# A convolution block's sums in the spare PSUM banks, two loads swapped, and five more warm-up transposes

## The chip, the cores and the metric

The kernel runs on one core of a Trainium2 chip. The metric is the device time of one execution in microseconds (us). The engines are TensorE (PE in the profile; its weight loads are PEld), VectorE (DVE), ScalarE (ACT), GpSimd (POOL) and SyncE (SP), which here only issues loads.

## What is computed

One layer of a hybrid encoder on a sequence of 256 rows and 2048 columns, in float32:

```python
xn = rms_norm(h, norm1_g)
proj = xn @ w_in                      # 2048 x 5120: q, k, v, and the convolution's ga, gg
...                                   # attention on q, k, v gives att
u = ga * sigmoid(gg)                  # 1024 channels
u = causal_depthwise_conv(u, conv_w, conv_b)      # 31 taps along the sequence
u = silu(layer_norm(u, conv_ln_g, conv_ln_b))
h = h + concat([att, u]) @ w_out
hn = rms_norm(h, norm2_g)
h = h + (silu(hn @ w_gate) * (hn @ w_up)) @ w_down
```

## The kernel before

**Products.** Each float32 matrix is cut into a rounded part (`hi`) and a rest (`lo`), and a product is the sum of three matmuls: hi by hi, hi of the weights by lo of x (lines 368 and 369), and lo of the weights by hi of x (line 374). A weight chunk is 512 KB. SP loads it (`raw`), ScalarE casts it to `whi` (line 329), and VectorE takes the difference as `wlo` (line 338). TensorE does the first half of a chunk from `whi` and the second from `wlo`.

**Blocks.** `w_in` is worked through in blocks of columns, each summed over all 2048 rows into two PSUM banks, one for each half of the 256 sequence rows. The first five blocks are those of the convolution: `CONV_BLOCKS = (1, 1, 2, 2, 2)` tiles of 128 channels, with both `gg` and `ga` columns. So blocks 1 and 2 have 256 columns and blocks 3 to 5 have 512. Block 1 has five chunks, block 2 four, block 3 eight.

**Banks.** PSUM has eight banks. Four are the pool `acc_ps`, from which blocks take two in turn (`accs[key]` in `multiply`). Four are the pool `aux_ps`, for transposes, attention scores and the like. `held` counts the banks of the second pool that are in longer use; whoever wants one waits with `room` until the count allows it. A block with `spare=True` takes its two banks from `aux_ps` and adds two to `held`. Before, only parts of the output projection did so, and block 3 followed block 1 in its two banks.

**What happens to a block's sums.** `glu_done` runs when a block is summed. It waits until the row norm of x (`rstd1`, from the squares of x on ScalarE, a reduction on VectorE in line 513 and a power on GpSimd in line 213) is known, takes the sigmoid of the `gg` half on ScalarE (line 539), and multiplies on VectorE (line 544, tile `u`). These two read the block's banks. Then TensorE transposes `u` (line 552), ScalarE copies it (line 553) and makes the first tap (line 557), and VectorE adds the other thirty (line 564).

**What sets the order.** The program is written out in order. Such followers are generators: `resume` lets each go one step, twice a chunk, so they stand in each engine's queue at fixed places between the chunks. `run_side` puts taps between the splits, by a budget of VectorE's time.

**The start.** ScalarE's queue issues the first part of x transposed (`xt`), then the norm columns (`cols`: gains and biases, 29 KB); SP's issues weights and the rest of x. ScalarE scales x by a column of `cols` (line 235, `lhi`), VectorE makes the rest (line 236, `llo`). Meanwhile TensorE transposes the identity matrix `WARM` times.

Of the kernel before, what the change touches and what calls it, by code (L numbers as in the profile page):

```python
# [22 lines left out]
NM = S // P  # L23
# [25 lines left out]

NK = 2  # L50

WARM = 14

XPARTS = (range(0, 2), range(2, 4), range(4, 8), range(8, 12), range(12, 16))

# [53 lines left out]
def tile_block(  # L109
# [6 lines left out]
    act, dve, pool, pe, sp = nc.scalar, nc.vector, nc.gpsimd, nc.tensor, nc.sync  # L116
# [23 lines left out]
    def warm_up(n):  # L140
        warm = aux_ps.tile([P, N], F32, tag="aux", name="ps_warm")
        for _ in range(n):
            pe.transpose(warm[:, :P], ident, ident)

    warm_up(WARM)

    cols = once.tile([P, NR], F32, tag="cols", name="cols")
    halves_of_x = [early.tile([P, HK, S], F32, tag="wb", name="xt") for _ in range(2)]

    def x_load(ks, queue):  # L150
        i, k = divmod(ks[0], HK)
        n = len(ks)
        queue.dma_start(out=halves_of_x[i][:, k : k + n].rearrange("p k s -> p (k s)"),
                        in_=xt[:, ks[0] * S : (ks[0] + n) * S])

    x_load(XPARTS[0], act)
    act.dma_start(out=cols, in_=gains)

    act.copy(small.tile([P, 8], F32, tag="rsq", name="first"), neghalf)

    def col(key, k):
        return cols[:, AT[key] + k : AT[key] + k + 1]
# [88 lines left out]
    def lag(n):  # L251
        for _ in range(n):
            yield


    held = [0]

    def room(n, hold=0):
        while held[0] + n > AUX:
            yield  # L260
        held[0] += hold
# [6 lines left out]
    def spend(us):  # L268
        credit[0] -= us
# [19 lines left out]
    def block(w, cols, ks, xs, done=None, bkey=None, first=True, last=True, spare=False, cuts=()):  # L289

        ks = list(ks)
        cols = [(cols, N)] if isinstance(cols, int) else cols
        width = sum(n for _, n in cols)
        bkey = bkey if bkey is not None else ("b", len(chunks))
        i = 0
        cuts = list(cuts)
        while i < len(ks):
            part = ks[i : i + (cuts.pop(0) if cuts else NK * N // width)]
            i += len(part)
            chunks.append(dict(w=w, k0=part[0], nk=len(part), cols=cols, width=width, xs=xs, bkey=bkey,  # L300
                               first=part[0] == ks[0] and first, last=last and i == len(ks),
                               done=done if i == len(ks) else None, spare=spare, by_dma=False,
                               load=load_chunk, round=round_chunk,
                               split=split_chunk, multiply=multiply))
# [222 lines left out]
        pool.memset(upad[b][:, :, : W - 1], 0.0)  # L527
    y = pre.tile([P, NCT, S], F32, tag="y", name="y", bufs=1)

    def glu_done(c0, nct, ps):  # L530

        w = nct * P
        while not normed:
            yield
        yield
        sig = []
        for m in range(NM):
            sig.append(pre.tile([P, HN], F32, tag="p1", name="sig"))
            act.activation(sig[m][:, :w], ps[m][:, :w], AF.Sigmoid, scale=rstd1[m])
        yield from lag(2)  # L540
        us = []
        for m in range(NM):
            u = pre.tile([P, HN], F32, tag="wt", name="u", bufs=4)
            dve.scalar_tensor_tensor(u[:, :w], ps[m][:, w:], rstd1[m], sig[m][:, :w], ALU.mult, ALU.mult)  # L544
            us.append(u)
        spend(0.25)
        yield from lag(3)
        yield from room(1)
        pt = aux_ps.tile([P, 2, S], F32, tag="aux", name="ps_u")
        for j in range(nct):  # L550
            for m in range(NM):
                pe.transpose(pt[:, j, m * P : (m + 1) * P], us[m][:, j * P : (j + 1) * P], ident)
        act.copy(upad[c0 // NB][:, c0 % NB : c0 % NB + nct, W - 1 :], pt[:, :nct])
        yield
        cts = range(c0, c0 + nct)
        for ct in cts:
            act.activation(y[:, ct, :], upad[ct // NB][:, ct % NB, :S], AF.Identity,
                           bias=col("cb", ct), scale=cw[:, ct, :1])
            side.append(deque((lambda k=k, ct=ct: tap(k, ct)) for k in range(1, W)))

    def tap(k, ct):
        src = upad[ct // NB][:, ct % NB, k : k + S]
        wk = cw[:, ct, k : k + 1]
        dve.scalar_tensor_tensor(y[:, ct, :], src, wk, y[:, ct, :], ALU.mult, ALU.add)  # L564
        if k == W - 1:
            tapped[ct // NB] += 1
            if tapped[ct // NB] == NB:
                start(conv_back(ct // NB))
# [647 lines left out]
    c0 = 0  # L1216
    for nct in CONV_BLOCKS:
        block("w_in", [(GC + c0 * P, nct * P), (AC + c0 * P, nct * P)], range(KD), fx,
              lambda ps, c0=c0, nct=nct: glu_done(c0, nct, ps), cuts=[len(p) for p in XPARTS] if c0 == 0 else ())
        c0 += nct  # L1220
    for b in range(2):
        block("w_in", KC + b * N, range(KD), fx, lambda ps, b=b: qk_done("k", b, ps))
# [67 lines left out]
```

## Time and profile before

| | us |
|---|---|
| median of 3 runs | 1061.22 (1060.52 to 1062.36) |
| the profiled execution: its time | 1062.85 |
| its span in the profile | 1061.1 |
| PE busy | 1036.1 (98%) |
| DVE busy | 882.1 (83%) |
| ACT busy | 667.4 (63%) |
| POOL busy | 138.1 (13%) |

A row of a time line gives the start in us from the span's start, the length in us, the engine, the line, the operation, what it writes and reads, and how many equal instructions the row joins (then the length runs from the first's start to the last's end). In brackets stands the idle time of the engine before it and what ended that. A row of a table by stretches gives each engine's busy time in the stretch with the number of its instructions in brackets, then the TensorE clock that was granted (PEclk, 1.00 is full), the DMA engines' busy share and what they moved in GB/s. A row of loads gives the median time from issue to landing at its end.

### The profile page before, as it was taken

To read this page: it belongs to the slowest core of one execution; us is meant where nothing else is said; L and a number is where in the kernel's file an instruction comes from. 1 tells how busy PE (TensorE), PEld (TensorE's weight loads), DVE (VectorE), ACT (ScalarE), POOL (GpSimd) and SP (SyncE) were. 2 spreads that over 40 slices of the span, in tenths; PEclk is the share of its full clock that TensorE was granted. 3 is DMA by queue.
4 is the path that set the end of the run, shared out by engine and by line. 5 is a ranking of instruction groups with operands and counts; after the bars stand their busy time and mean duration, and the time that the engine had idled before them with its cause. 6 is when DMAs were issued, how large, how long until landed. Compare 5 with 4: busy or idle time off the path is not lost.

```text
span 1061.1 us, 13189 instructions
## 1 busy us (share of the span) xinstructions
PE 1036.1 (98%) x4734; PEld 856.6 (81%) x4734; DVE 882.1 (83%) x1103; ACT 667.4 (63%) x850; POOL 138.1 (13%) x182
## 2 busy tenths in 40 slices
PE   8799999999999999999999999999999999999998
PEld 8688888878778887787888888888888888888776
DVE  5499999989766489989979679899896697989984
ACT  6554457756567466676765566775865556668661
POOL 0030022211200100010101120100101111001021
PEclk9899999999999999999999999999999999999999
DMA  9556555454546668987969998979878999879985
GB/s 361 204 170 200 193 180 171 159 170 147 164 155 198 213 211 257 310 235 231 321 196 292 283 301 265 293 212 324 238 238 259 297 280 333 244 233 275 282 219 117
DMA packets 63186, 250.20 MB, mean 236 GB/s; under 512 B 7184, under 2 KB 8208, under 8 KB 55696
## 3 DMA queue, kind: packets, MB, share of 16 engines
q1 hardware_dynamic: 48224, 201.34, 53.2%
q0 software_dynamic: 14608, 47.72, 23.2%
q8 instruction: 37, 0.61, 0.2%
q10 hardware_dynamic: 288, 0.29, 0.1%
q14 instruction: 29, 0.24, 0.1%
HBM read 240.94 MB, written 8.39 MB: 235 GB/s over the span
## 4 chain that ended last, share of the span: by engine, by line
PE 55%; DVE 6%; issue 2%; ACT 1%; DMA 0%; POOL 0%; DVEq 0%; ACTq 0%; POOLq 0%
PE q L1069 10%; PE q L1070 10%; PE q L1074 10%; PE q L1048 8%; PE q L1049 7%; PE q L1050 7%; DVE wl L1031 1%; DVE wl L1030 1%; DVE wt L1019 1%; PE ps_a L886 1%; DVE wlo L338 1%; PE acc L374 1%; PE acc L369 1%; PE acc L368 1%; DVE wt L1020 0%
## 5 line engine op out<-in xcount | busy, mean ns | idle before, releaser
L329 ACT CAST whi<-raw 128x1024 fp32r<-128x1024 f32 (+1 forms) x261 | 268.8, 1046 | 114.5 <-PE q L1070 48.5
L338 DVE TENSOR_TENSOR wlo<-raw,whi 128x1024 fp32r<-128x1024 f32 (+1 forms) x188 | 227.4, 1217 | 97.5 <-ACT whi L329 97.4
L368 PE MATMUL acc<-whi,lhi 128*128 128x512 f32 (+1 forms) x448 | 169.5, 383 | 9.6 <-DVE u L544 6.9
L369 PE MATMUL acc<-whi,llo 128*128 128x512 f32 (+1 forms) x448 | 167.4, 379 | 0.0
L1026 ACT CAST wh<-wt 128x2048 fp32r<-128x2048 f32 x58 | 110.8, 1910 | 38.1 <-DVE wt L1021 37.8
L1031 DVE TENSOR_TENSOR wl<-wt,wh 128x2048 fp32r<-128x2048 f32 x58 | 132.7, 2287 | 1.8 <-ACT wh L1026 0.9
L333 POOL DMA_DIRECT2D wlo<-in_wts_dram x73 | 63.9, 875 | 521.8 <-ACT wlo L332 480.4
L1030 DVE TENSOR_TENSOR wl<-wb,wh 128x1536 fp32r<-128x1536 f32 x58 | 101.7, 1753 | 29.6 <-ACT wh L1025 29.4
L1069 PE MATMUL q<-whi,chi 128*128 128x512 f32 x320 | 125.3, 392 | 0.0
L1070 PE MATMUL q<-whi,clo 128*128 128x512 f32 x320 | 124.6, 389 | 0.0
L374 PE MATMUL acc<-wlo,lhi 128*128 128x512 f32 (+1 forms) x448 | 115.2, 382 | 1.5 <-DVE wlo L338 1.5
L1048 PE MATMUL q<-wh,fhi 128*128 128x512 f32 x280 | 109.8, 392 | 3.1 <-DVE sum L1150 1.4
L1050 PE MATMUL q<-wl,fhi 128*128 128x512 f32 x280 | 109.0, 389 | 0.0
L1049 PE MATMUL q<-wh,flo 128*128 128x512 f32 x280 | 109.0, 389 | 0.0
L368 PEld LDWEIGHTS acc<-whi,lhi 128*128 128x128 f32 x448 | 86.0, 192 | 25.3 <-issue 7.0
L564 DVE SCALAR_TENSOR_TENSOR y<-upad,cw,y 128x256 f32<-128x256 f32 x240 | 103.2, 481 | 0.3
L369 PEld LDWEIGHTS acc<-whi,llo 128*128 128x128 f32 x448 | 86.0, 192 | 15.0
L1025 ACT CAST wh<-wb 128x1536 fp32r<-128x1536 f32 x58 | 85.5, 1474 | 18.0 <-PE q L1049 9.9
L374 PEld LDWEIGHTS acc<-wlo,lhi 128*128 128x128 f32 x448 | 80.7, 191 | 16.8 <-DVE wlo L338 2.4
L1074 PE MATMUL q<-wlo,chi 128*128 128x512 f32 x320 | 86.3, 391 | 0.0
L332 ACT ACTIVATE wlo<-raw 128x1024 fp32r<-128x1024 f32 x73 | 77.2, 1057 | 0.0
L1019 DVE TENSOR_TENSOR wt<-wb 128x1024 f32<-128x1024 f32 x58 | 70.8, 1220 | 0.9 <-DMA wb<-in_wts_dram 0.4
(208 smaller groups left out, 1679.8 us busy)
## 6 DMA issues: line engine op xcount, KB each, us to landing
raw<-in_wts_dram SPq DMA_DIRECT2D x259, 512.0 KB, 5.4
wb<-in_wts_dram SPq DMA_DIRECT2D x57, 1024.0 KB, 7.5
wlo<-in_wts_dram POOLq DMA_DIRECT2D x73, 512.0 KB, 9.0
out_dram<-sum POOLq DMA_DIRECT2D x22, 256.0 KB, 7.0
h<-in_x_dram SPq DMA_DIRECT2D x4, 512.0 KB, 8.8
out_dram<-h POOLq DMA_DIRECT2D x8, 256.0 KB, 5.5
xt<-in_xt_dram SPq DMA_DIRECT2D x3, 512.0 KB, 7.4
wb<-in_wts_dram POOLq DMA_DIRECT2D x1, 1024.0 KB, 8.0
```

The costliest lines, as they stand in the source:

```text
L329: act.copy(c["hi"], c["raw"])
L338: dve.tensor_tensor(c["lo"], c["raw"], c["hi"].bitcast(F32), ALU.subtract)
L368: pe.matmul(ps[m], xhi[:, ms], hi[:, j, :], start=c["first"] and j == 0, stop=False)
L369: pe.matmul(ps[m], xlo[:, ms], hi[:, j, :], start=False, stop=False)
L374: pe.matmul(ps[m], xhi[:, ms], lo[:, j, :], start=False, stop=c["last"] and j == nk - 1)
L1031: dve.tensor_tensor(c["lo"][:, :4], c["t"], c["hi"][:, :4].bitcast(F32), ALU.subtract)
L1048: pe.matmul(ps, fhi[:, f, p, :], c["hi"][:, w], start=bool(first), stop=False)
L1049: pe.matmul(ps, flo[:, f, p, :], c["hi"][:, w], start=False, stop=False)
L1050: pe.matmul(ps, fhi[:, f, p, :], c["lo"][:, w], start=False, stop=bool(last))
L1069: pe.matmul(ps, plain[i][0][:, ms], hi[:, i, :], start=i == 0 and bool(c["first"].get(qs[m])), stop=False)
L1070: pe.matmul(ps, plain[i][1][:, ms], hi[:, i, :], start=False, stop=False)
L1074: pe.matmul(sum_bank(c, qs[m]), plain[i][0][:, ms], lo[:, i, :], start=False, stop=i == 1 and bool(c["last"].get(qs[m])))
```

## The change

Three things. Block 3 (`c0 == 2`) gets `spare=True`: it sums in two banks of `aux_ps`, and `glu_done` gives these back in `held` once `u` is written. ScalarE's queue issues the norm columns ahead of the first part of x. `WARM` is 19 in place of 14.

```diff
-WARM = 14
+WARM = 19
...
+    act.dma_start(out=cols, in_=gains)
     x_load(XPARTS[0], act)
-    act.dma_start(out=cols, in_=gains)
...
-    def glu_done(c0, nct, ps):
+    def glu_done(c0, nct, ps, spare):
...
             us.append(u)
+        if spare:
+            held[0] -= NM
         spend(0.25)
...
         block("w_in", [(GC + c0 * P, nct * P), (AC + c0 * P, nct * P)], range(KD), fx,
-              lambda ps, c0=c0, nct=nct: glu_done(c0, nct, ps), cuts=[len(p) for p in XPARTS] if c0 == 0 else ())
+              lambda ps, c0=c0, nct=nct: glu_done(c0, nct, ps, c0 == 2),
+              cuts=[len(p) for p in XPARTS] if c0 == 0 else (), spare=c0 == 2)
```

On every engine the instructions stand in the same order as before, but for the swapped loads and the number of warm-ups; what changes are the banks and with them the waits. (Lines behind the change have numbers higher by 2 or 3.) The head of ScalarE's queue, before (-) and now (+):

```order
-L1281 UNCONDITIONAL_BRANCH
+L1284 UNCONDITIONAL_BRANCH
+L156 DMA cols<-in_gains_dram 128x58
 L153 DMA xt<-in_xt_dram 128x512
-L157 DMA cols<-in_gains_dram 128x58
 L159 ACT_TABLE_LOAD
 L159 COPY first<-neghalf 128x8
```

The two loads have changed places, and nothing else has moved there. TensorE's queue where block 2 ends and block 3 begins, with the engines that an instruction waits for in brackets (`acc_324` and `acc_325` are block 2's banks, `acc_481` and `acc_482` block 3's, which before are those of block 1); before:

```order
L374 MATMUL acc_324<-wlo_363,lhi_90 128x256 [waits DVE_49]
L374 MATMUL acc_324<-wlo_363,lhi_90 128x256 x3
L374 MATMUL acc_325<-wlo_363,lhi_90 128x256 x4
L368 MATMUL acc_481<-whi_399,lhi_90 128x512 [waits DVE_49,PE_49,Activation_49]
L369 MATMUL acc_481<-whi_399,llo_91 128x512
L368 MATMUL acc_482<-whi_399,lhi_90 128x512 [waits DVE_49,PE_49,Activation_49]
L369 MATMUL acc_482<-whi_399,llo_91 128x512
```

The same place now (block 2 has `acc_329` and `acc_330`, block 3 `acc_486` and `acc_487`):

```order
L374 MATMUL acc_329<-wlo_368,lhi_90 128x256 [waits DVE_49]
L374 MATMUL acc_329<-wlo_368,lhi_90 128x256 x3
L374 MATMUL acc_330<-wlo_368,lhi_90 128x256 x4
L368 MATMUL acc_486<-whi_404,lhi_90 128x512 [waits Activation_49]
L369 MATMUL acc_486<-whi_404,llo_91 128x512
L368 MATMUL acc_487<-whi_404,lhi_90 128x512
L369 MATMUL acc_487<-whi_404,llo_91 128x512
```

Block 3's first matmul waited for VectorE and ScalarE, and its first in the second bank again; now the first waits for ScalarE alone, whose cast it reads. Two chunks later stand the transposes of block 1's `u`, here with the end of block 3's second chunk ahead of them and the start of its third behind; before:

```order
L374 MATMUL acc_481<-wlo_445,lhi_90 128x512 x2
L374 MATMUL acc_482<-wlo_445,lhi_90 128x512 x2
L552 MATMUL ps_u_521<-ident_85,u_491 128x128
L552 MATMUL ps_u_521<-ident_85,u_493 128x128
L368 MATMUL acc_481<-whi_477,lhi_90 128x512 [waits Activation_49]
```

And now:

```order
L374 MATMUL acc_486<-wlo_450,lhi_90 128x512 [waits DVE_49]
L374 MATMUL acc_486<-wlo_450,lhi_90 128x512
L374 MATMUL acc_487<-wlo_450,lhi_90 128x512 x2
L554 MATMUL ps_u_526<-ident_85,u_496 128x128 [waits DVE_49]
L554 MATMUL ps_u_526<-ident_85,u_498 128x128 [waits DVE_49]
L368 MATMUL acc_486<-whi_482,lhi_90 128x512 [waits Activation_49]
```

The transposes stand where they stood, but each now waits for VectorE itself, since nothing ahead of it on TensorE has waited for its `u`.

## The prediction

> **What bounds the kernel now.** I read the shares of busy time first, then the table of waits for TensorE, then the time line of each engine around the one long wait.
>
> ```profile
> span 1061.1 us, 13189 instructions
> PE 1036.1 (98%) x4734; PEld 856.6 (81%) x4734; DVE 882.1 (83%) x1103; ACT 667.4 (63%) x850; POOL 138.1 (13%) x182
> ...
> PE acc L368 <- DVE u L544: 6.9, 1, 6.9
> ...
> PE acc L374 <- DVE wlo L338: 1.5, 2, 1.2
> PE q L1048 <- DVE sum L1150: 1.4, 2, 0.9
> ```
>
> TensorE (PE) sets the end: it is busy for 1036.1 of 1061.1 us. Of the 25 us that it idles, one wait of 6.9 us stands out: a matmul of line 368 waits for `u`, which VectorE writes in line 544 (the columns are the sum of the waits, their number and the longest). In TensorE's time line:
>
> ```profile
> 31.11 1.12 PE L374 MATMUL acc<-wlo,lhi 128*128 128x256 f32 x8
> 39.10 0.77 PE L368 MATMUL acc<-whi,lhi 128*128 128x512 f32 x1 [6.87 <-DVE u L544]
> 44.36 0.63 PE L368 MATMUL acc<-whi,lhi 128*128 128x512 f32 x1
> 47.37 0.38 PE L552 MATMUL ps_u<-ident,u 128*128 128x128 f32 x2
> 47.51 0.48 PE L368 MATMUL acc<-whi,lhi 128*128 128x512 f32 x1
> ...
> 56.04 0.39 PE L368 MATMUL acc<-whi,lhi 128*128 128x512 f32 x1
> 58.76 0.39 PE L368 MATMUL acc<-whi,lhi 128*128 128x512 f32 x1
> ```
>
> The row at 31.11 ends block 2. Its eight matmuls follow each other by 0.12 us (1.12 less the 0.28 of one, over 7), so the next could start at 32.07. Block 3 starts at 39.10. Its first chunk takes 5.26 us (39.10 to 44.36), its second 3.01 (to 47.37), and then come the transposes of block 1's `u`. Later a chunk takes 2.72 us (56.04 to 58.76), so the first two chunks lose 5.26 + 3.01 - 5.44 = 2.83 us more. The granted clock (PEclk) says why:
>
> ```profile
> core 0: us, PE busy (x) PEld busy (x) DVE busy (x) ACT busy (x) POOL busy (x), PEclk, DMA share, GB/s
> 31.24:34.66 3.42, 0.99 (x9) 0.78 (x7) 2.49 (x4) 2.95 (x3) 1.19 (x2) 1.00 0.79 283
> 34.66:44.90 10.24, 5.80 (x14) 4.59 (x15) 3.49 (x6) 3.22 (x6) 1.27 (x3) 0.50 0.59 198
> 44.90:47.40 2.50, 2.50 (x13) 1.99 (x12) 0.00 (x0) 0.00 (x0) 0.00 (x0) 1.00 0.00 0
> ...
> 225.80:229.22 3.42, 2.48 (x13) 2.07 (x14) 3.42 (x6) 0.80 (x2) 0.00 (x0) 1.00 0.44 143
> ```
>
> It is 0.50 from 34.66 to 44.90 and 1.00 on both sides, so it stays low until 5.8 us after the work resumed. The wait costs 6.87 + 2.83 = 9.7 us in this execution.
>
> **What ends the wait.** Here are the rows of ScalarE, VectorE and GpSimd that lead to it and follow it.
>
> ```profile
> 23.27 1.05 ACT L329 CAST whi<-raw 128x1024 fp32r<-128x1024 f32 x1 [2.75 <-DMA raw<-in_wts_dram]
> ...
> 30.94 1.98 ACT L329 CAST whi<-raw 128x1024 fp32r<-128x1024 f32 x2
> 36.40 1.03 ACT L329 CAST whi<-raw 128x1024 fp32r<-128x1024 f32 x1
> 39.59 1.03 ACT L329 CAST whi<-raw 128x1024 fp32r<-128x1024 f32 x1
> 47.79 0.37 ACT L553 COPY upad<-ps_u 128x256 f32<-128x256 f32 x1 [7.16 <-PE ps_u L552]
> ...
> 32.00 1.23 DVE L338 TENSOR_TENSOR wlo<-raw,whi 128x1024 fp32r<-128x1024 f32 x1 [2.60 <-ACT whi L329]
> 33.14 0.21 DVE L513 TENSOR_REDUCE ss<-ss 128x1 f32<-128x4 f32 x2
> 37.47 1.23 DVE L338 TENSOR_TENSOR wlo<-raw,whi 128x1024 fp32r<-128x1024 f32 x1 [2.98 <-ACT whi L329]
> 38.61 0.60 DVE L544 SCALAR_TENSOR_TENSOR u<-acc,rstd,sig 128x128 f32<-128x128 f32 x2
> 41.80 0.60 DVE L544 SCALAR_TENSOR_TENSOR u<-acc,rstd,sig 128x128 f32<-128x128 f32 x2
> 50.29 2.56 DVE L564 SCALAR_TENSOR_TENSOR y<-upad,cw,y 128x256 f32<-128x256 f32 x5
> ...
> 35.55 0.55 POOL L213 TENSOR_TENSOR rstd<-rsq,neghalf 128x1 f32<-128x1 f32 x1
> ```
>
> A weight chunk lands late, and the cast at 23.27 has waited 2.75 us for it. ScalarE then works without a gap, through the squares of x, to 32.92. VectorE's reduction at 33.14 and GpSimd's power up to 36.10 give `rstd`; sigmoid, a cast and a split follow, and `u` is written from 38.61 to 39.21. None of this waits for work that TensorE does after 32.07.
>
> **The change, part by part.**
>
> *The third block in the other banks.* Its first matmul then waits for its cast alone. The two casts from 30.94 are block 3's first two. The first of them is done when the split at 32.00 starts, so TensorE goes on at 32.07. Two chunks at 2.72 bring it to 37.51. The split of the second chunk comes behind the reductions, which end at 33.35, and takes 1.2 us like the others: it is done by 34.6, ahead of the chunk's second half at about 36.6 (34.79 and eight of its twelve matmuls). Then come, in the same order as before, the transposes of block 1's `u`, and these need both halves of it. The two writes take 0.60 us together, so the first half is there when block 3 started before, at 39.10, and the second some 0.25 later. So a wait stays: 37.67 (a last matmul ends 0.16 after the next could start: 39.10 less 6.87 is 32.23) to 39.10, 1.43 us, plus 0.2 between the two transposes. Behind the waiting transpose stands the third chunk, which starts at about 39.4 in place of 47.51. That is 8.1 us earlier. By parts: 6.87 + 2.83 - 1.43 - 0.2 = 8.1.
>
> What is late next? The third chunk's cast is done at 37.43 and its split at 38.70, in time. The fourth chunk starts at 42.1, and its cast is done at 40.62. Block 2's transposes come at about 43.9, and their `u` is done at 42.40. ScalarE copies the transposed `u` behind the cast that ends at 40.62, so at 40.6 in place of 47.79. VectorE's taps (line 564) start at about 43.4 in place of 50.29: they gain 6.9 where TensorE gains 8.1, so VectorE's lead shrinks by 1.2. From there VectorE has no idle time to make up for it:
>
> ```profile
> 50.00:120.00 70.00, 70.00 (x317) 57.96 (x316) 69.86 (x125) 32.66 (x43) 9.70 (x14) 1.00 0.56 187
> 120.00:140.00 20.00, 20.00 (x90) 16.52 (x89) 17.65 (x31) 14.10 (x33) 5.40 (x6) 1.00 0.61 204
> ...
> 67.93 1.21 DVE L338 TENSOR_TENSOR wlo<-raw,whi 128x1024 fp32r<-128x1024 f32 x1
> ...
> 71.46 1.07 PE L374 MATMUL acc<-wlo,lhi 128*128 128x512 f32 x4
> ```
>
> (The third number after the stretch's length is VectorE: 69.86 of 70.00.) The smallest lead that I find in this stage is that of the chunk whose split ends at 69.14 and whose second half starts at 71.46: 2.32 us. With 1.2 less, 1.1 us are left, so TensorE still doesn't wait. Between 120 and 140 VectorE idles for 2.35 us, which gives the lead back ahead of the two waits for `wlo` (1.5 us together). Of the waits after that the largest in sum is 1.4 us, on a sum of the products just made (line 1150); those follow TensorE and move with it.
>
> *The norm columns first.* ScalarE's first work waits for them:
>
> ```profile
> 1.35 3.25 PE L143 MATMUL ps_warm<-ident 128*128 128x128 f32 x14 [1.35 <-POOL neghalf L137]
> 7.33 0.58 PE L368 MATMUL acc<-whi,lhi 128*128 128x256 f32 x1 [2.73 <-ACT whi L329]
> 5.86 0.91 ACT L235 ACTIVATE lhi<-xt,cols 128x256 fp32r<-128x256 f32 x2 [2.73 <-DMA cols<-in_gains_dram]
> 9.18 1.04 ACT L329 CAST whi<-raw 128x1024 fp32r<-128x1024 f32 x1 [0.57 <-DMA raw<-in_wts_dram]
> ...
> xt<-in_xt_dram ACTq DMA_DIRECT2D x1, 256.0 KB, 4.2
> cols<-in_gains_dram ACTq DMA_DIRECT2D x1, 29.0 KB, 4.6
> raw<-in_wts_dram SPq DMA_DIRECT2D x2, 256.0 KB, 4.4
> ```
>
> Columns and x swap places on ScalarE's queue, where the second is issued some 0.4 us after the first (the columns' 5.86 less 4.6 is 1.2 or a little less; x at 0.7). x then lands at about 1.2 + 4.2 = 5.4, and the start moves from 5.86 to 5.4. The gain is 0.4 at most; it could also be a loss, if x is held up behind SP's loads. Either way it ends at 9.18, where ScalarE waits for a weight chunk, and ScalarE's waits there and at 23.27 (0.57 + 2.75 = 3.3 us) would hide a loss. I take nothing.
>
> *Five more warm-up transposes.* Fourteen take 3.25 us, 0.22 each, so nineteen end at 5.7. TensorE's first matmul comes at 6.9 at the earliest (7.33 less 0.4). They delay nothing. What they could gain is clock in the first chunks, and whatever TensorE gains ahead of 37.51 is lost in the wait for `u` until 39.10. So I take nothing; the ends are nothing on both sides, by that 1.4 us of cover. If the cover is gone (`u` 1.4 us earlier), each would count in full.
>
> The sum is 8.1 us. The profiled execution took 1062.85 us (span 1061.1 and 1.75 around it), 1.63 over the median of 1061.22, so against itself it would come to 1054.75. Against the median it is 1053.1.
>
> **How far the size may be off.** What I know least is the cold share, 2.83 us in the one execution profiled. With none of it the gain would be 5.3; if the second chunk too had run as slowly as the first (5.26), 10.3. The runs of before lie between 1060.52 and 1062.36, 1.84 us apart, and a cold share that differed by more would show there. So I keep 8.1 with 0.9 on either side: 1052.2 to 1054.0.
>
> The Trainium skill (TensorE: Matmul & The Clock Gate, "The HAM clock gate") says that the gate judges activity in free-running windows of about 3.41 us and goes back to full clock after a busy one. The drop and the rise lie 10.24 us apart, three such windows, so the trace agrees. By that rule the low clock after the wait would last 3.4 to 6.8 us, by chance, and the gain would be 5.3 + 1.7 to 5.3 + 3.4: an estimate of 7.0 to 8.7, about the same range.
>
> **Rivals.**
> - *The clock drops in the wait that stays.* It dropped in a wait of 6.87 us and not in the one of 1.2 us near 226 (row 225.80, PEclk 1.00). The new one, 1.4 to 1.7 us, is far nearer to the second. If it drops as it did here, up to the same 2.83 are lost: 1053.1 + 2.8 = 1055.9. Chance 0.1. The Trainium skill (the same page, "HAM oscillation") warns of idle gaps over some 3.4 us only; by that rule this case is out, and no run here shows a gap between 1.2 and 6.9.
> - *VectorE becomes the bound in the taps.* It decides if the taps move by less than 8.1 - 2.3 = 5.8 us. For it: 69.86 of 70 us busy. Against it: their release moves by 6.9. One more cast and split ahead of them (1.03 + 1.23) would cost 2.26 - 1.1 = 1.2, so 1054.3; if they didn't move at all, the gain would be the lead of 2.3 alone, 1058.9. Chance 0.05.
> - *Slower: x lands late.* Swapped behind the columns, the first part of x could queue behind what SP issues by then. Beyond 5.9 its delay first uses up ScalarE's 3.3 us of waits, then moves `u` one for one, and it takes 8.1 + 2.1 more until the time is 0.2% over: a landing at about 19.4. At 21 the time would be 1064.9. Against it: SP's own small loads land 4.4 us after their issue, so 5.6 rather. Chance 0.01.
> - *It doesn't do what it says*: something else holds block 3 until 39.1, and the time stays at 1061.2. But only its cast is left as a wait, and that is done by 32.0. Chance 0.02.
>
> **The numbers.** The forecast as worked out has 0.82, 1053.1 with its own range. The low end goes 0.1 below that; the high end, 1055.2, takes in VectorE's smaller case and the drop of the clock where it costs less than the full 2.8; what lies beyond holds under 0.15. About 0.2% (2.1 us) is what a measurement can tell from no change. Faster by more than that: the first three cases, 0.97; within it: 0.02; slower: 0.01.
>
> **What would show it.** In the changed kernel's time line the first matmul of block 3 stands at about 32.1; the transposes of block 1's `u` wait some 1.4 us for VectorE and start at 39.1; the next chunk starts at 39.4 and a chunk from there takes 2.72. The granted clock stays at 1.00 from 31 to 48. The taps start at about 43.4. ScalarE's first work is at 5.4, its cast of the third chunk still at 9.2. TensorE's waits for `wlo` are still 1.5 us. I would be wrong if `u` isn't ready at 39.2 (the chain from the landing at 23.2 moved), if PEclk falls behind 41.5, or if new waits for `wlo` stand between 60 and 120.

## The result, and the profile after

The changed kernel takes 1054.38 us (median of 6 runs, 1054.01 to 1054.97), the kernel before 1061.17 (6 runs). The ratio is 0.9936 with a 95% interval of 0.9923 to 0.9949: faster by 6.8 us, where 8.1 were forecast (1053.1, range 1052.1 to 1055.2). Two repeats gave 1054.17 and 1054.23 against 1061.60 and 1061.39, ratios 0.9931 (0.9919 to 0.9944) and 0.9930 (0.9916 to 0.9944). The profiled execution took 1054.38 us, 8.5 less than the profiled one of before; why the two gaps differ is taken up below.

The page's head and TensorE's table of waits now:

```profile
span 1052.6 us, 13200 instructions
PE 1035.2 (98%) x4739; PEld 855.6 (81%) x4739; DVE 881.8 (84%) x1103; ACT 667.8 (63%) x850; POOL 138.6 (13%) x182
...
PE acc L368 <- ACT whi L329: 1.3, 1, 1.3
PE ps_u L554 <- DVE u L544: 1.3, 1, 1.3
PE acc L374 <- DVE wlo L338: 1.2, 1, 1.2
```

TensorE does the same work (1035.2 against 1036.1 us; five transposes more, less time at the low clock). The wait of 6.9 us for `u` has become one of 1.3, and it now stands at the transposes. (The one of 1.3 for `whi` is the program's start.) TensorE's time line shows the order of events:

```profile
30.86 1.12 PE L374 MATMUL acc<-wlo,lhi 128*128 128x256 f32 x8
31.89 0.50 PE L368 MATMUL acc<-whi,lhi 128*128 128x512 f32 x1
34.75 0.39 PE L368 MATMUL acc<-whi,lhi 128*128 128x512 f32 x1
38.89 0.59 PE L554 MATMUL ps_u<-ident,u 128*128 128x128 f32 x2 [1.25 <-DVE u L544]
39.23 0.48 PE L368 MATMUL acc<-whi,lhi 128*128 128x512 f32 x1
42.08 0.39 PE L368 MATMUL acc<-whi,lhi 128*128 128x512 f32 x1
45.05 0.39 PE L368 MATMUL acc<-whi,lhi 128*128 128x512 f32 x1
```

Block 3's first two chunks run from 31.89 on, where TensorE stood still before; then it waits 1.25 us, and the third chunk starts at 39.23 in place of 47.51. The stretch around it, with the columns as before (PEclk is the third number from the end):

```profile
31.00:48.00 17.00, 15.74 (x74) 12.63 (x73) 11.55 (x20) 12.62 (x18) 2.46 (x4) 1.00 0.61 213
```

The clock stays at full. The other engines at the places that the prediction named:

```profile
5.45 0.91 ACT L235 ACTIVATE lhi<-xt,cols 128x256 fp32r<-128x256 f32 x2 [2.31 <-DMA xt<-in_xt_dram]
8.93 1.04 ACT L329 CAST whi<-raw 128x1024 fp32r<-128x1024 f32 x1 [0.73 <-DMA raw<-in_wts_dram]
23.14 1.05 ACT L329 CAST whi<-raw 128x1024 fp32r<-128x1024 f32 x1 [2.75 <-DMA raw<-in_wts_dram]
40.41 0.37 ACT L555 COPY upad<-ps_u 128x256 f32<-128x256 f32 x1
...
38.49 0.60 DVE L544 SCALAR_TENSOR_TENSOR u<-acc,rstd,sig 128x128 f32<-128x128 f32 x2
43.34 2.56 DVE L566 SCALAR_TENSOR_TENSOR y<-upad,cw,y 128x256 f32<-128x256 f32 x5
60.98 1.21 DVE L338 TENSOR_TENSOR wlo<-raw,whi 128x1024 fp32r<-128x1024 f32 x1
...
63.21 1.07 PE L374 MATMUL acc<-wlo,lhi 128*128 128x512 f32 x4
```

ScalarE starts at 5.45 in place of 5.86, waiting for x and no longer for the columns, and waits 0.73 and 2.75 us for weight chunks (0.57 and 2.75 before). `u` is written at 38.49 (38.61 before), the taps begin at 43.34. VectorE's lead at the narrow place that the prediction named (the split of 60.98 ends at 62.19, the chunk's second half starts at 63.21) is 1.02 us, 2.32 before: still a lead. A narrower one stands later, among the last taps:

```profile
166.01 1.22 DVE L338 TENSOR_TENSOR wlo<-raw,whi 128x1024 fp32r<-128x1024 f32 x1
...
167.74 1.07 PE L374 MATMUL acc<-wlo,lhi 128*128 128x512 f32 x4
```

This split ends at 167.23, so 0.51 us are left (1.33 before, from 174.55 to 175.88).

### The profile page after: what moved, and what is told of

Read it like the earlier page. It is cut to its first block, busy times and chain, and to the rows that moved or that the text cites. A ratio compares the mean times of both kernels' runs of the same rounds, so it can differ in the third digit from the quotient of the medians.

```text
span 1052.6 us, 13200 instructions
## 1 busy us (share of the span) xinstructions
PE 1035.2 (98%) x4739; PEld 855.6 (81%) x4739; DVE 881.8 (84%) x1103; ACT 667.8 (63%) x850; POOL 138.6 (13%) x182
## 4 chain that ended last, share of the span: by engine, by line
PE 57%; DVE 7%; issue 1%; ACT 1%; POOL 0%; DVEq 0%; POOLq 0%; ACTq 0%
PE q L1071 10%; PE q L1072 10%; PE q L1076 10%; PE q L1050 8%; PE q L1052 8%; PE q L1051 8%; DVE wl L1033 1%; PE acc L369 1%; PE acc L374 1%; PE acc L368 1%; DVE wt L1021 1%; DVE wlo L338 1%; DVE wl L1032 1%; PE ps_a L888 1%; DVE wt L1022 1%
```

## The experiments

**The cold share from execution to execution.** The kernel before, run again.

> The kernel before, unchanged, for each run's time and granted clock. The change gained 8.5 us between the two profiled executions (1062.85 to 1054.38) but 6.8 between the medians (1061.17 to 1054.38). Theory: the low clock behind the wait of 6.9 us lasts differently long from run to run, so the runs spread by up to 1.7 us, a run with more low clock is the slower one, and the first profiled execution (clock 0.995, 10.2 us low, 2.8 lost) was one of the dear ones; the usual share lost is then about 1.5 us. Rival: the excess of that execution came from elsewhere; then all runs show the clock at 0.995 and spread without regard to it.

It took 1061.42 us (11 runs, 1060.54 to 1063.35; ratio to the other runs of before 0.9997, 0.9988 to 1.0006). This time the profiled execution was a cheap one, 1060.54. Its rows, and the clock in the stretch around the wait and behind it:

```profile
37.65 0.60 DVE L544 SCALAR_TENSOR_TENSOR u<-acc,rstd,sig 128x128 f32<-128x128 f32 x2
...
38.15 0.77 PE L368 MATMUL acc<-whi,lhi 128*128 128x512 f32 x1 [5.79 <-DVE u L544]
45.80 0.48 PE L368 MATMUL acc<-whi,lhi 128*128 128x512 f32 x1
...
35.51:42.34 6.83, 4.20 (x10) 3.37 (x11) 3.49 (x6) 2.52 (x5) 0.00 (x0) 0.50 0.46 159
42.34:45.70 3.36, 3.36 (x16) 2.70 (x16) 0.00 (x0) 0.00 (x0) 0.00 (x0) 1.00 0.32 127
```

Two things differ from the first profile. The low clock lasted 6.83 us, not 10.24, so the two chunks with their transposes took 7.65 us (38.15 to 45.80) where it was 8.41 (39.10 to 47.51): 0.76 less of cold share, 2.1 where it was 2.8. (The profile of the start alone, below, has the banks of before too and gives a third value: 7.58 us, from 38.72 to 46.30, or 2.0.) And `u` came 0.96 us earlier, with the loads ahead of it. The other 0.6 lie late in the program: the second half of a chunk that starts at 400.70 in the first profile starts at 398.99 in this one, 1.71 earlier, which is no more than the two together. So against this execution the first was dear on all three counts, the cold share among them.

That the granted clock would tell cheap runs from dear ones did not show: the clock of single runs (0.993 to 0.997 in this comparison) doesn't order their times, 10 runs at 0.995 had a median of 1061.1 and 21 at 0.997 one of 1061.4. Only the three at 0.993 and 0.994 are all dear, 1062.6 to 1063.4. The figure is a poor measure of this wait: it counts low clock in the first 14 us too, where the waits for loads cover it, and not even all of that. In the first profile matmuls of block 1 start 0.21 us apart up to 10.70 and 0.12 apart from 10.85 on, half pace at first, while the clock given for that time is 1.00.

**The banks alone.** `WARM = 14`, and the loads in the old order:

```diff
-WARM = 19
+WARM = 14
-    act.dma_start(out=cols, in_=gains)
     x_load(XPARTS[0], act)
+    act.dma_start(out=cols, in_=gains)
```

> The change without the swapped loads and with 14 warm-ups: only block 3's banks. Theory: the whole gain is here, so 1054.2 to 1054.8, with the transposes of block 1's u at about 39.0 behind a wait of 1.2 to 1.5 us. Rival: the earlier start gives a part; then 1055 or more.

1054.19 us, ratio 0.9928 (0.9915 to 0.9942): the whole gain. TensorE and VectorE:

```profile
32.44 0.40 PE L368 MATMUL acc<-whi,lhi 128*128 128x512 f32 x1
39.32 0.59 PE L554 MATMUL ps_u<-ident,u 128*128 128x128 f32 x2 [1.25 <-DVE u L544]
...
38.92 0.60 DVE L544 SCALAR_TENSOR_TENSOR u<-acc,rstd,sig 128x128 f32<-128x128 f32 x2
```

**The start alone.** The kernel before with `WARM = 19` and the columns ahead of x.

> The kernel before with the swapped loads and 19 warm-ups, banks as before. Theory: ScalarE starts 0.4 us earlier, the gain is gone at its wait for the third weight chunk (about 9) and at the later one at 23, and u is written at 38.6 as before: 1061.0, the wait for u 6.9 to 7.2 us. Rival: the start carries through, 0.4 us or more: 1060.7 or less; or a warmer first stretch adds to it: 1059.

1061.99 us, ratio 1.0003 (0.9994 to 1.0011): no difference. In its profile x landed late enough that ScalarE did not even start earlier, so this profile can't show what becomes of an earlier start:

```profile
5.98 0.91 ACT L235 ACTIVATE lhi<-xt,cols 128x256 fp32r<-128x256 f32 x2 [2.84 <-DMA xt<-in_xt_dram]
9.54 1.05 ACT L329 CAST whi<-raw 128x1024 fp32r<-128x1024 f32 x1 [0.81 <-DMA raw<-in_wts_dram]
...
PE acc L368 <- DVE u L544: 6.1, 1, 6.1
```

**The clock kept up through the old wait.** The kernel before, with matmuls whose sums are not used, ahead of block 3's first:

```diff
+BUSY = 28
...
+        if c["first"] and c is chunks[9]:
+            busy = aux_ps.tile([P, N], F32, tag="aux", name="ps_busy")
+            xhi, _ = operand(c["xs"], c["k0"])
+            for _ in range(BUSY):
+                pe.matmul(busy, xhi[:, :P], hi[:, 0, :], start=True, stop=True)
```

> The kernel before with 28 more matmuls of 128x512 (0.23 us each, 6.4 us, from the chunk's own cast, into a spare bank, their sums unused) ahead of block 3's first matmul: TensorE is busy through most of the wait, and the wait's end stays. Theory (the low clock comes from the idle time): block 3 starts at 39.1 at full clock, the transposes come at 44.6 in place of 47.4, the granted clock stays 1.00, the runs spread less than before's; the time falls by the usual share lost, 1.5 us, to 1059.6. Rival (every run loses the 2.8 of the profiled one): 1058.3. Rival (the low clock has nothing to do with the idle time): 1061.2.

```profile
32.47 6.54 PE L370 MATMUL ps_busy<-whi,lhi 128*128 128x512 f32 x28
38.84 0.39 PE L375 MATMUL acc<-whi,lhi 128*128 128x512 f32 x1
44.29 0.38 PE L559 MATMUL ps_u<-ident,u 128*128 128x128 f32 x2
...
31.00:48.00 17.00, 17.00 (x84) 14.29 (x83) 7.89 (x13) 8.38 (x13) 2.47 (x4) 1.00 0.52 187
...
37.80 0.60 DVE L551 SCALAR_TENSOR_TENSOR u<-acc,rstd,sig 128x128 f32<-128x128 f32 x2
```

1059.47 us, ratio 0.9982 (0.9974 to 0.9991), 2.0 us below before, and a spread of 1.5 us (2.8 over the 11 runs of before above). The clock stays at 1.00 and the two chunks take 5.45 us (38.84 to 44.29). So about 2.0 us of the old wait's price were the low clock, and idle time of TensorE is its cause. It may be a little more: with `u` as early as here, at 37.80, block 3 could have started at 38.3, and the added matmuls held it until 38.84.

**How far ahead the transposes stand.** What the changed kernel gains should be the work that stands ahead of block 1's transposes. In `glu_done`, for block 1 alone, one of these three lines in each run (the remarks behind them are added here):

```diff
-        yield from lag(3)
+        yield from lag(1 if c0 == 0 else 3)    # one chunk earlier
+        yield from lag(2 if c0 == 0 else 3)    # half a chunk earlier
+        yield from lag(4 if c0 == 0 else 3)    # half a chunk later
```

> The changed kernel with block 1's transposes a chunk earlier in TensorE's queue, ahead of block 3's second chunk. They wait for the same u (38.5 to 39.1), now from 34.8, 4.1 us, and one chunk less runs in the wait. Theory (the gain is the work that stands ahead of the transposes): 2.7 us slower than the changed kernel, 1057.1, if the clock holds. If a wait of 4.1 us lowers the clock, as one of 5.8 to 6.9 did, 1 to 2.5 us more: 1058 to 1059.6. Rival (where they stand doesn't count, the wait for u is hidden elsewhere): 1054.4.

1058.70 us (10 runs), ratio 0.9973 (0.9964 to 0.9982): 4.5 more than the changed kernel beside it (1054.17). A chunk that no longer runs in the wait is 2.7; what is left, 1.8, is put down to low clock, which is back for 6.83 us:

```profile
38.68 0.73 PE L554 MATMUL ps_u<-ident,u 128*128 128x128 f32 x2 [3.67 <-DVE u L544]
39.07 0.78 PE L368 MATMUL acc<-whi,lhi 128*128 128x512 f32 x1
44.34 0.49 PE L368 MATMUL acc<-whi,lhi 128*128 128x512 f32 x1
...
37.70:44.53 6.83, 5.85 (x15) 4.62 (x16) 4.32 (x10) 4.31 (x7) 0.00 (x0) 0.50 0.37 128
```

In this execution the chunk behind the wait takes 5.27 us (39.07 to 44.34) in place of 2.72, so the low clock cost it some 2.6, more than the 1.8 between the medians. The division of the 4.5 is right only to within some 0.8.

> The changed kernel with block 1's transposes half a chunk earlier, ahead of the second half of block 3's second chunk: the wait is 2.2 us long and four matmuls (0.9 us) less run in it. Theory: 0.9 us slower than the changed kernel, 1055.3, with the clock at 1.00 behind the wait. Rival (2.2 us already lowers the clock): 1056.5 or more, and PEclk at 0.50 in the chunks behind the wait.

1056.14 us, ratio 0.9948 (0.9936 to 0.9961), 2.0 more than the changed kernel. The five runs lie at 1055.1 and 1055.2 (clock 1.000), 1056.1 and 1056.3 (0.998) and 1057.6 (0.997). The first two are the theory's 0.9 us over the changed kernel, and their clock leaves no room for a low stretch behind the start (3.41 us at half clock would make it 0.998). The profiled one is the run of 1056.1, and in it a wait of 2.0 us has lowered the clock:

```profile
38.68 0.59 PE L554 MATMUL ps_u<-ident,u 128*128 128x128 f32 x2 [1.99 <-DVE u L544]
...
35.97:39.38 3.41, 1.42 (x8) 0.80 (x7) 1.75 (x3) 1.77 (x5) 0.00 (x0) 1.00 0.48 154
39.38:42.79 3.41, 3.41 (x10) 2.63 (x9) 2.43 (x5) 3.38 (x5) 0.00 (x0) 0.50 0.47 172
42.79:47.00 4.21, 4.21 (x21) 3.42 (x20) 4.10 (x7) 0.67 (x2) 0.00 (x0) 1.00 0.57 208
```

The whole wait lay in one stretch of 3.41 us, in which TensorE was busy for 1.42; the next such stretch ran at half clock. The run of 1056.3 looks like it by time and clock, and that of 1057.6 as if it had been low for longer, but neither has a profile. For comparison the changed kernel was run beside these, and once more with the last two below:

> The changed kernel again, beside the three that follow. Expected 1054.2 to 1054.6, spread about 1 us, clock 0.998 to 1.000, as before.

> The changed kernel once more, beside the next two: 1054.0 to 1054.6.

These are the 1054.17 and 1054.23 above.

**Half a chunk later, to take the last wait away.**

> The changed kernel with block 1's transposes half a chunk later in TensorE's queue (behind the first half of block 3's third chunk). Theory (the wait that is left costs only because the transposes stand ahead of work that is ready): the wait of 1.25 us is gone, and the third chunk runs in it, so 1054.4 - 1.4 = 1053.0. VectorE's smallest lead in the taps, 1.0 us, falls by up to 1.4, so up to 0.4 may be given back: 1053.0 to 1053.4. Rival (VectorE is already the bound of the taps): no gain, 1054.2 or more, with waits for wlo between 55 and 75 us.

> The version with block 1's transposes half a chunk later, repeated to size its gain: the first time 0.6 us lay between the medians, where the profiles, counted from the writing of u, showed 1.07. Theory (u's own time scatters by 1 us between executions and hid a part): 1053.0 to 1053.5, 0.6 to 1.1 below the changed kernel. Rival (VectorE took it back): 0.3 or less below it.

1053.54 us (0.9923, 0.9910 to 0.9937) and in the repeat 1054.65 (0.9933, 0.9920 to 0.9946); the changed kernel beside them took 1054.17 and 1054.23. Both forecasts of a gain were missed: the first, 1053.4 at most, by 0.1, the second, 0.6 to 1.1 below the changed kernel, with 0.4 above it. The wait is gone in the profile, yet most of its gain doesn't arrive. Of the later transposes (first) and of the changed kernel beside them (second), the writing of block 1's `u`, the first tap, and the start of a chunk late in this part of the program:

```profile
38.91 0.60 DVE L544 SCALAR_TENSOR_TENSOR u<-acc,rstd,sig 128x128 f32<-128x128 f32 x2
43.77 0.48 DVE L566 SCALAR_TENSOR_TENSOR y<-upad,cw,y 128x256 f32<-128x256 f32 x1
...
44.09 0.40 PE L368 MATMUL acc<-whi,lhi 128*128 128x512 f32 x1
310.19 0.39 PE L368 MATMUL acc<-whi,mchi 128*128 128x512 f32 x1
...
PE acc L368 <- DVE mchi L631: 1.0, 1, 1.0
```

```profile
38.44 0.60 DVE L544 SCALAR_TENSOR_TENSOR u<-acc,rstd,sig 128x128 f32<-128x128 f32 x2
43.29 1.00 DVE L566 SCALAR_TENSOR_TENSOR y<-upad,cw,y 128x256 f32<-128x256 f32 x2
...
310.37 0.39 PE L368 MATMUL acc<-whi,mchi 128*128 128x512 f32 x1
...
PE acc L368 <- DVE mchi L631: 0.6, 1, 0.6
```

`u` itself comes 0.47 us later in the first of these executions, so times are compared from `u` on. Block 3's fifth chunk starts 5.18 us after `u` (44.09) where the changed kernel's takes 6.56 (45.05 less 38.49, in its first profile): 1.38 gained, as expected. The chunk at 310 starts 271.28 against 271.93 after `u`: 0.65 is left. The taps begin 4.86 and 4.85 after `u`: VectorE gains nothing there, and its lead at the split near 167 us falls to 0.05 (it ends at 166.77, the second half starts at 166.82). TensorE waits for the convolution's output (`mchi`) 1.0 us in place of 0.6, which is 0.4 of the 0.7 that is lost. That VectorE is late with all of it is not so: counted from `u`, the first piece of `mchi` is cast 1.30 us earlier than in the changed kernel, the last is done 1.06 later, in another order. What takes the other 0.3 is not shown. The repeat's profile has 0.67 left, against the same profile of the changed kernel. In the times this is within what scatters: ten runs of it have a median of 1054.0, sixteen of the changed kernel 1054.3. Faster than the changed kernel it is not shown to be.

> The later transposes with the old start (x ahead of the norm columns, 14 warm-ups). Without the wait for u nothing on TensorE covers the start any more. Theory (block 3's first chunk then waits for its cast, which hangs on ScalarE's wait for a weight chunk near 23 us and not on the start): the same as the version with the new start within 0.3 us. Rival (the start was hidden by the wait for u alone): 0.3 to 0.5 us slower than it.

1053.39 us (0.9923, 0.9909 to 0.9937). The old start is no slower, even with no wait for `u` to cover it. The forecast, within 0.3 us of the new start, fits the first measurement of that (1053.54) and not the second beside it (1054.65); the two measurements of one kernel are 1.1 apart, so nothing finer can be read from this.

## Why the prediction was right, and where its size was off

The mechanism held step by step. Block 3 started at 31.89 (32.1 forecast), the wait at the transposes was 1.25 us (1.43), the third chunk started at 39.23 (39.4), 8.3 us earlier than in the first profile (8.1). The banks alone gave everything, the start nothing. The gain was not eaten later: the two profiled spans differ by 8.5 (1061.1 and 1052.6), hardly more than the 8.3 gained here, and in between the lead holds: the chunk half that starts at 400.70 before starts at 392.28 now, 8.4 earlier.

VectorE's lead fell to 1.02 us, forecast 1.1, with no new wait for `wlo`. But the tightest place was not where the prediction looked: it took the lead as given back between 120 and 140 us, and 0.51 is all that stayed near 167. The clock did not drop in the wait that stayed. The reason that I gave, that 1.4 us is near a wait of 1.2 and far from one of 6.9, was thin: the experiment shows that 2.0 us can be enough, where all of it falls into one stretch of 3.41, also against the rule that the prediction set beside this rival. The kernel was nearer to that edge than the chance of 0.1 was argued from. (The prediction's words that no gap between 1.2 and 6.9 is on show pass over its own row at 7.33, a wait of 2.73 us. It decides nothing, since matmuls ahead of it too, the warm-ups, ran 0.22 us apart where later transposes of that size are 0.13 apart.)

What was off is the term for the cold share. I took the 2.83 us of the one execution that was profiled, and set its sum against the median. Keeping TensorE busy through the old wait showed 2.0 as the usual share, and two more profiles with the old banks 2.1 and 2.0. With 5.3 (stall less the wait that stays) and 2.0 the gain comes to 7.3, and the comparisons gave 6.8 to 7.4. The forecast's own range of 1052.2 to 1054.0 missed for that; the stated range, widened for other cases that did not come, held 1054.38, and that it did was luck. The prediction also argued that a cold share much off would show in the spread of its three runs, 1.84 us; over more runs before lay between 1060.15 and 1064.14. I had seen that the profiled run lay 1.63 us over the median and did not ask which term had made it dear. About half of that was this one, 2.8 where 2.0 to 2.1 is usual. Its `u`, at 38.61, was not a late one among the profiles; against the second profile up to 0.6 more came behind 400 us, from what is not known.

## What to carry to other kernels

A wait for banks can be moved behind work that is ready. The gain here was about the work that stands ahead of the instruction that still needs the late result, and the low clock that the long wait had brought: half a chunk less there cost 0.9 us where the clock held, a chunk less 4.5 with the clock. Half a chunk more is not shown to gain anything, and half of its lead was lost to other waits on the way. Before pricing a stall with the low clock behind it from one profile, look whether that execution is a typical one; its distance to the median of the runs is the warning. And an earlier start was worth nothing here, where later waits for loads stand behind it.

## What the runs showed of the hardware that I had not expected

A wait of 2.0 us lowered the clock for 3.41 us (the run of half a chunk earlier). In that profile TensorE had been busy for 1.42 of 3.41 us (42%) in the window ahead. In the changed kernel's profile its 1.25 us of waiting did not lower it, nor in three more profiles with this wait (1.24 to 1.27 us), nor in the kernel before a stretch with 2.48 of 3.42 (73%). The low stretches behind the waits measured here last 3.41, 6.83 and 10.24 us, one, two and three times the same window; the Trainium skill has the clock decided window by window as well (TensorE: Matmul & The Clock Gate, "Part 1: The HAM clock gate").

Thirteen profiles of these kernels wrote block 1's `u` between 37.65 and 38.92 us. In all of them that is 15.3 to 15.4 us after the cast near 23 us, and this cast had waited 1.5 to 2.9 us for a weight chunk: the landing of one load sets `u`. The spread of 1.3 us is nearly what the changed kernel's sixteen runs differ by (1.5).
